# The loop over further token tiles of the experts moves from behind the first gather to behind the last expert

## The chip, the core and the metric

The kernel runs on one core of one Trainium2 chip. The metric is the device time of one execution in microseconds, of which the median over several runs is compared. The engines are TensorE (PE; its weight loads are PEld), VectorE (DVE), ScalarE (ACT), GpSimd (POOL) and SyncE (SP). [...]

## What is computed

Two blocks in a row, on 512 tokens of 1024 features. The first block has two layers: attention (a sliding window in layer 0, latent attention in layer 1), LayerNorm, a mixture of 32 experts, LayerNorm. The second block is a latent stream with a context stream beside it. The mixture is what matters here:

```python
def hier_moe(x, w_group, w_expert, w_gate, w_up, w_down):
    ...
    expert = (g_idx * M_PER_GROUP + e_idx).reshape(-1)      # two experts for each token
    order = jnp.argsort(expert)
    sizes = jnp.bincount(expert, length=M_EXPERTS)
    xs = xt[tok_sorted]
    hid = jax.nn.silu(lax.ragged_dot(xs, w_gate, sizes)) * lax.ragged_dot(xs, w_up, sizes)
    ys = lax.ragged_dot(hid, w_down, sizes) * weight
    return jax.ops.segment_sum(ys, tok_sorted, num_segments=n_tok)
```

512 tokens times 2 experts make 32 tokens for an expert on average.

## The kernel before

`moe(i, ...)` runs one mixture, for layer i = 0 and 1, and `_moe` is its body. The router's results on VectorE give, for each expert, the ranks of its tokens (`rkm`) and their number (`n_e`). Each expert has one tile of 64 token slots; two experts make a pair, and a loop over p = 0 to 15 works off the pairs. `ahead(p)` finds the token of each slot: one-hot matrices `oh` (L699, VectorE), small matmuls (L702), a sum and an addition (L706, L710) into `slots`, and a gather of the rows from DRAM (`xd`) into `x` on POOL (L756). `turn` transposes the rows (L767) and copies them to `xg` (L768). `gate_up` (L806), `turn_hidden` (L815) and `down` (L825) compute the experts, and `add_rows` (L742, POOL) adds their rows to `acc` in DRAM. The weights of a pair are twelve loads on SP (L863) into wide buffers `wx`, early ones `we`, spare ones `ws`, or granules `w`, a ring of three buffers of 512 KB that the other stages use too.

An expert with more than 64 tokens needs further tiles. Their number over all experts is `nov` (L783). Each engine reads it into a register (L892) and runs a loop that often (L893); its body finds the tile, gathers its rows and the expert's weights with indirect loads, and computes it. The loop closes a basic block on all five engines: what was traced ahead of it stands ahead of it in each queue, and what was traced behind it stands behind. Within a block a scheduler orders the instructions of each engine by a timeline of its own.

`meanwhile()` is the context stream, whose steps `fill` puts between the experts, on the right side of the memory, with its loads on POOL (L187). When the pairs are done, `acc` is read back as four row tiles (L979), and `combine` adds LayerNorm (L997, L305 to L309) and hands each tile on: in layer 0 to `mla_down`, which transposes it (L253) and multiplies with `b_w_down` (loaded at L189, split into two parts on ScalarE, L235, and VectorE, L236); in layer 1 to the second block, which transposes it at L1124 and multiplies with `w_in`.

```python
        ixs = []
        rows = [ahead(0)]                       # the first gather
        ...
        loaded = weights_of(0)
        ...
        with self.after("Pool")():
            n_over = nc.values_load(nov[0:1, 0:1], min_val=0, max_val=15)
        with tc.For_i(0, n_over, 1):
            ...
        rows += [ahead(p) for p in range(1, 3)]
```

Of the kernel before, what the change touches and what calls it, by code (L numbers as in the profile page):

```python
# [104 lines left out]
def bcast_rows(ap, n, parts=128):  # L105

    return bass.AP(tensor=ap.tensor, offset=ap.offset, ap=[[0, parts], [1, n]])


def finished(steps):  # L110

    while True:
        try:
            next(steps)
        except StopIteration as end:
            return end.value
# [13 lines left out]
class Net:  # L130
# [498 lines left out]
    def _moe(self, i, lg, meanwhile):  # L629
        nc, ins, tc = self.nc, self.ins, self.tc  # L630
# [109 lines left out]
        def add_rows(ix, y):  # L740

            nc.gpsimd.indirect_dma_start(out=acc, out_offset=bass.IndirectOffsetOnAxis(ap=ix, axis=0), in_=y, in_offset=None,  # L742
                                         bounds_check=1023, oob_is_err=False, compute_op=ALU.add)

        def targets_of(a, b):
            ix, w = targets([rkm[:, :, e] for e in range(a, b)], put[:, :, a:b], gone[:, a:b])
            return {e: (ix[:, e - a:e - a + 1], w[:, e - a:e - a + 1]) for e in range(a, b)}
# [3 lines left out]
        def rows_of(ix, n, rows=None):  # L751

            if rows is None:
                rows = ring.pop(0)
                ring.append(rows)
            nc.gpsimd.indirect_dma_start(out=rows[:n], out_offset=None, in_=self.xd,  # L756
                                         in_offset=bass.IndirectOffsetOnAxis(ap=ix[:n], axis=0), bounds_check=511,
                                         oob_is_err=False)
            return rows

        def turn(rows, n):

            xg = self.lp.tile([128, 8, 128], F32, name="xg")
            for g in range(2):
                ps = self.bank("tp", [128, 4, 128])
                for k in range(4):
                    nc.tensor.transpose(ps[:, k, :n], rows[:n, 4 * g + k::8], self.ident[:n, :n])  # L767
                (V.tensor_copy if g else nc.scalar.copy)(xg[:, 4 * g:4 * g + 4, :n], ps[:, :, :n])  # L768
            return xg

        def ahead(p):
            a = 1 if 0 < p < 4 else p // 4 * 4
            if a == p:
                b = 1 if p == 0 else p // 4 * 4 + 4
                ixs.append(slots([rkm[:, :, 2 * q:2 * q + 2] for q in range(a, b)], 2, past[:, a:b]))
            return rows_of(ixs[-1][:, p - a:p - a + 1], 128)


        more, ov, nof, nov = sm([128, 7, 32], "more"), sm([128, 32], "ov"), sm([128, 1], "nof"), sm([128, 1], "nov", I32)
# [18 lines left out]
        rows = [ahead(0)]  # L798

        def gate_up(hid, j, xg, wg, wu):  # L800

            ps = self.bank("sc")
            own, other = (slice(64 * a, 64 * a + 64) for a in (j, 1 - j))
            for k, ws in enumerate(zip(wg, wu)):
                for r, w in zip((other, own), ws):
                    nc.tensor.matmul(ps[r], xg[:, k], w, start=k == 0, stop=k == 7)  # L806
            nc.scalar.activation(hid[own], ps[other], AF.Silu)  # L807
            V.tensor_tensor(hid[own], hid[own], ps[own], op=ALU.mult)  # L808

        def turn_hidden(hid, rows=slice(0, 128)):  # L810

            n = rows.stop - rows.start
            tp = self.bank("tp", [128, 4, 128])
            for k in range(4):
                nc.tensor.transpose(tp[:, k, :n], hid[rows, k::4], self.ident[rows, rows])  # L815
            hT = self.lp.tile([128, 4, 128], F32, name="hT")
            V.tensor_copy(hT[:, :, :n], tp[:, :, :n])  # L817
            return hT

        def down(hT, wd, weight):  # L820

            py = self.bank("mm")
            for k, w in enumerate(wd):
                for h in range(2):
                    nc.tensor.matmul(py[64 * h:64 * h + 64], hT[:, k], w[:, 512 * h:512 * h + 512], start=k == 0, stop=k == 3)  # L825
            y = self.lp.tile([128, 512], F32, name="y")
            nc.scalar.activation(y, py, AF.Copy, scale=weight)  # L827
            return y

        def hidden():  # L830
            return self.lp.tile([128, 512], F32, name="hid")

        es = ExitStack()
# [18 lines left out]
        def weights_of(p):  # L852

            both = [([], [], []) for _ in range(2)]
            for j, n, h in [(j, n, h) for j in range(2) for h in range(2) for n in (0, 1)] + [(j, 2, h) for j in range(2) for h in range(2)]:
                e, ws = 2 * p + j, both[j]
                src, kk = ((w_g, 8), (w_u, 8), (w_d, 4))[n]
                parts, when = stream([128, kk // 2, 4096 // kk])
                k = h * kk // 2
                for w in parts:  # L860
                    m = w.shape[1]
                    with when():
                        nc.sync.dma_start(w, src[e].rearrange("(p k) f -> p k f", k=kk)[:, k:k + m])  # L863
                    k += m
                    ws[n].extend(w[:, a] for a in range(m))
            return both
# [2 lines left out]
        self.nstream = -1  # L869
        base, first, gen = (4, 99, 17) if i else (0, 6, 11)  # L870
        loaded = weights_of(0)

        tau = sm([128, 1], "tau")
        V.memset(tau, -1.0)
        oe, ob = sm([128, 32], "oe"), sm([128, 32], "ob")
# [12 lines left out]
        in_parts(put, we, tmp)  # L888
        past_half(gone, n_e)

        with self.after("Pool")():
            n_over = nc.values_load(nov[0:1, 0:1], min_val=0, max_val=15)  # L892
        with tc.For_i(0, n_over, 1):  # L893
            V.tensor_scalar(tau, tau, 1.0, None, op0=ALU.add)
            tiles_up_to(oe, ob)
# [19 lines left out]
            xg = turn(rows_of(slots([rko], 1)[:, 0:1], 64, self.granule([128, 1024])), 64)  # L915
# [15 lines left out]
            to, weight = targets([rko[:, :, 0]], one, go)  # L931
            hid = hidden()
            gate_up(hid, 1, xg[:, :, :64], picked("moe_w_gate", 8), picked("moe_w_up", 8))
            add_rows(to, down(turn_hidden(hid, slice(64, 128))[:, :, :64], picked("moe_w_down", 4), weight))
        rows += [ahead(p) for p in range(1, 3)]
        beside = meanwhile()
        instructions = nc.cur_bb.bb.instructions

        def fill(n):

            k = len(instructions)
            while n > 0:
                if next(beside, self) is self:
                    break
                n -= sum(a.engine == mybir.EngineType.PE for a in instructions[k:])
                k = len(instructions)

        for p in range(16):
            if p < 13:
                rows.append(ahead(p + 3))  # L950
            xg = turn(rows[p], 128)
            ws = weights_of(p) if p else loaded
            if p == 0:
                to = targets_of(0, 2)
            hid = hidden()
            for j in range(2):
                gate_up(hid, j, xg[:, :, 64 * j:64 * j + 64], *ws[j][:2])
            hT = turn_hidden(hid)
            for j in range(2):
                at, weight = to[2 * p + j]  # L960
                add_rows(at, down(hT[:, :, 64 * j:64 * j + 64], ws[j][2], weight))
                if p > 1:
                    fill(70 if i == 0 else 72)
            if p == 1 or (p == 0 and i == 0):
                es.close()
            if p == 0:
                to |= targets_of(2, 8)
            elif p % 4 == 3 and p < 15:
                to = targets_of(2 * p + 2, 2 * p + 10)
        loaded, added = self.after("SP"), self.after("Pool")  # L970
        finished(beside)
        xs, lnp = self.new_x(), self.wide([128, 2, 1024])
        with loaded():
            lnp = [lnp[:, a] for a in range(2)]
            for w, nm in zip(lnp, ("ln_g", "ln_b")):
                nc.sync.dma_start(w, bcast_rows(ins[nm][i, 1], 1024))
        for t, x in enumerate(xs):
            with added():
                nc.gpsimd.dma_start(x, self.acc[i][128 * t:128 * t + 128])  # L979
            added = self.after("Pool")  # L980
        return xs, lnp

    def wide(self, shape):
# [941 lines left out]
```

## Time and profile before

| what | value |
|---|---|
| three runs | 3419.17, 3430.11 and 3430.08 us; median 3430.08 |
| the profiled execution: its time | 3424.68 us |
| the profiled execution: its span | 3422.9 us |
| TensorE busy | 3139.3 us, 92% of the span |
| VectorE, ScalarE, POOL busy | 48%, 34%, 12% of the span |
| mean granted clock of TensorE | 0.959 of full speed |
| experts of layer 0, with their entry and exit | about 282 to 939 us |
| experts of layer 1, with their entry and exit | about 1210 to 1994 us |

All times of the trace count from the span's start. A row of the timeline has its start, its length, the engine (SPq is SP's queue), the line, the operation, what it writes and reads, and in brackets how long the engine had been idle and what ended that.

### The profile page before, as it was taken

Reading aid. Unit: us, or ns where it says so; the run is one execution under the profiler, and the core shown is the slowest. Engines: PE = TensorE matmul, PEld = TensorE weight load, DVE = VectorE, ACT = ScalarE, POOL = GpSimd, SP = SyncE. Lnnn points to the kernel's source line nnn. Section 1 sums busy time; section 2 is a strip of 40 time slices with the busy share of each in tenths; the row PEclk is TensorE's granted clock in tenths of the full one; section 3 lists DMA queues with packets and bytes.
Section 4 is the critical chain, followed back from the end, with each engine's and each line's share of the span. In section 5 each row is a group of like instructions: output and inputs, shape, how many; then the busy total and the mean of one; then the engine's idle time right before and its main releaser. Section 6 shows DMA issues by size and latency. Waiting matters only on the chain. (4 is left out here: it accounts for less than half of the span.)

```text
span 3422.9 us, 46600 instructions
## 1 busy us (share of the span) xinstructions
PE 3139.3 (92%) x17508; PEld 2123.4 (62%) x17508; DVE 1655.5 (48%) x4015; ACT 1172.2 (34%) x2322; POOL 406.2 (12%) x538
## 2 busy tenths in 40 slices
PE   8997999999699969999889759999999999999998
PEld 5454445544286636666445257767888777678887
DVE  3454242223266645555423056565555556755555
ACT  3331222222255324333122044344342442543332
POOL 0000221212100013232121100130000000400000
PEclk9998999999899979999999979999999999999999
DMA  8779989999931469888898932223233232333331
GB/s 287 264 272 351 352 327 338 364 355 388 329 121 43 165 225 379 317 321 314 302 359 322 387 99 80 76 74 111 87 99 98 81 92 67 81 100 93 97 94 56
DMA packets 282686, 716.01 MB, mean 209 GB/s; under 512 B 34936, under 2 KB 164008, under 8 KB 234584
## 3 DMA queue, kind: packets, MB, share of 16 engines
q1 hardware_dynamic: 250008, 634.80, 51.4%
q0 software_dynamic: 32448, 78.18, 7.4%
q8 instruction: 140, 2.29, 0.3%
q14 instruction: 90, 0.74, 0.1%
HBM read 691.76 MB, written 37.87 MB: 213 GB/s over the span
## 5 line engine op out<-in xcount | busy, mean ns | idle before, releaser
L236 DVE TENSOR_TENSOR wl<-w,wh 128x1024 fp32r<-128x1024 f32 (+4 forms) x467 | 437.1, 950 | 276.9 <-ACT wh L235 271.9
L235 ACT CAST wh<-w 128x1024 fp32r<-128x1024 f32 (+4 forms) x467 | 377.5, 827 | 512.5 <-PE po L242 116.2
L806 PE MATMUL sc<-wx,xg 128*64 128x512 f32 x1416 | 473.0, 613 | 23.1 <-DMA wx<-in_moe_w_up 16.9
L240 PE MATMUL mm<-xTh,wh 128*128 128x512 f32 (+1 forms) x672 | 263.3, 392 | 11.6 <-ACT xTh L235 6.1
L806 PEld LDWEIGHTS sc<-wx,xg 128*64 128x64 f32 x1416 | 133.0, 139 | 222.4 <-issue 176.9
L242 PE MATMUL mm<-xTh,wl 128*128 128x512 f32 (+1 forms) x672 | 262.2, 390 | 0.9 <-DVE wl L236 0.9
L241 PE MATMUL mm<-xTl,wh 128*128 128x512 f32 (+1 forms) x672 | 260.0, 387 | 0.0
L808 DVE TENSOR_TENSOR hid<-hid,sc 64x512 f32<-64x512 f32 x64 | 43.8, 685 | 304.7 <-ACT hid L807 304.4
L825 PE MATMUL mm<-wx,hT 128*64 128x512 f32 x704 | 173.7, 625 | 10.5 <-DVE hT L817 5.5
L807 ACT ACTIVATE hid<-sc 64x512 f32<-64x512 f32 x64 | 37.8, 591 | 382.5 <-PE sc L806 382.3
L806 PE MATMUL sc<-w,xg 128*64 128x512 f32 x352 | 168.0, 610 | 0.0
L742 POOL DMA_INDIRECT acc<-y,to x64 | 106.9, 1671 | 462.9 <-ACT y L827 262.1
L240 PEld LDWEIGHTS mm<-xTh,wh 128*128 128x128 f32 x672 | 127.9, 190 | 43.0 <-ACT xTh L235 6.6
L241 PE MATMUL sc<-xTl,wh 128*128 128x512 f32 (+1 forms) x384 | 146.0, 380 | 0.0
L242 PEld LDWEIGHTS mm<-xTh,wl 128*128 128x128 f32 x672 | 127.8, 190 | 28.8 <-DVE wl L236 1.3
L240 PE MATMUL sc<-xTh,wh 128*128 128x512 f32 (+1 forms) x384 | 145.6, 379 | 0.0
L242 PE MATMUL sc<-xTh,wl 128*128 128x512 f32 (+1 forms) x384 | 145.1, 378 | 0.0
L241 PEld LDWEIGHTS mm<-xTl,wh 128*128 128x128 f32 x672 | 127.7, 190 | 26.9 <-issue 0.7
L240 PE MATMUL a<-xTh,wh 128*128 128x256 f32 (+2 forms) x472 | 139.6, 296 | 4.7 <-ACT rs L1449 0.9
L240 PE MATMUL po<-wh,gTh 128*128 128x512 f32 x352 | 137.9, 392 | 3.8 <-DVE t2k L1771 2.8
L241 PE MATMUL po<-wl,gTh 128*128 128x512 f32 x352 | 137.1, 390 | 0.0
L242 PE MATMUL po<-wh,gTl 128*128 128x512 f32 x352 | 136.3, 390 | 0.0
(518 smaller groups left out, 6702.7 us busy)
## 6 DMA issues: line engine op xcount, KB each, us to landing
wx<-in_moe_w_up SPq DMA_DIRECT2D x89, 1024.0 KB
wx<-in_moe_w_down SPq DMA_DIRECT2D x88, 1024.0 KB
wx<-in_moe_w_gate SPq DMA_DIRECT2D x88, 1024.0 KB
g<-in_w_ada SPq DMA_DIRECT2D x48, 1024.0 KB
w<-in_ffn_w_up SPq DMA_DIRECT2D x176, 256.0 KB
w<-in_moe_w_gate SPq DMA_DIRECT2D x60, 512.0 KB
w<-in_ffn_w_up POOLq DMA_DIRECT2D x88, 256.0 KB
w<-in_ffn_w_down SPq DMA_DIRECT2D x44, 512.0 KB
```

Source lines behind the costliest of these rows:

```text
L235: self.nc.scalar.copy(hi, src)
L236: self.nc.vector.tensor_tensor(lo, src, hi.bitcast(F32), op=ALU.subtract)
L240: mm(ps, ah, bh, start=start, stop=False)
L241: mm(ps, ah, bl, start=False, stop=False)
L242: mm(ps, al, bh, start=False, stop=stop)
L742: nc.gpsimd.indirect_dma_start(out=acc, out_offset=bass.IndirectOffsetOnAxis(ap=ix, axis=0), in_=y, in_offset=None, bounds_check=1023, oob ...
L806: nc.tensor.matmul(ps[r], xg[:, k], w, start=k == 0, stop=k == 7)
L807: nc.scalar.activation(hid[own], ps[other], AF.Silu)
L808: V.tensor_tensor(hid[own], hid[own], ps[own], op=ALU.mult)
L825: nc.tensor.matmul(py[64 * h:64 * h + 64], hT[:, k], w[:, 512 * h:512 * h + 512], start=k == 0, stop=k == 3)
```

## The change

The loop, its reading of `nov` and the tensors of its body move as one block. They stood behind `past_half(gone, n_e)`, ahead of the second and third gather and of all experts; they now stand behind the last expert, behind the end of the context stream (`finished(beside)`) and the loads of the LayerNorm parameters, and ahead of the read-back of `acc`. The register load loses its place behind POOL's last instruction, and the four read-backs theirs (`added`). The body is the same word for word.

```diff
-        with self.after("Pool")():
-            n_over = nc.values_load(nov[0:1, 0:1], min_val=0, max_val=15)
-        with tc.For_i(0, n_over, 1):
-            V.tensor_scalar(tau, tau, 1.0, None, op0=ALU.add)
...
         rows += [ahead(p) for p in range(1, 3)]
         beside = meanwhile()
...
-        loaded, added = self.after("SP"), self.after("Pool")
+        loaded = self.after("SP")
         finished(beside)
         xs, lnp = self.new_x(), self.wide([128, 2, 1024])
         with loaded():
             lnp = [lnp[:, a] for a in range(2)]
             for w, nm in zip(lnp, ("ln_g", "ln_b")):
                 nc.sync.dma_start(w, bcast_rows(ins[nm][i, 1], 1024))
+
+        n_over = nc.values_load(nov[0:1, 0:1], min_val=0, max_val=15)
+        with tc.For_i(0, n_over, 1):
+            V.tensor_scalar(tau, tau, 1.0, None, op0=ALU.add)
...
         for t, x in enumerate(xs):
-            with added():
-                nc.gpsimd.dma_start(x, self.acc[i][128 * t:128 * t + 128])
-            added = self.after("Pool")
+            nc.gpsimd.dma_start(x, self.acc[i][128 * t:128 * t + 128])
         return xs, lnp
```

In the rows of the changed kernel the loop has the lines L933 and L934, the read-back L977, the store of a row tile L997.

VectorE at the entry of layer 0, before, from the one-hot of the first gather (`nov` is the number of further tiles, `slots` the gather's row numbers, `put` the routing weights for the adds):

```order
L699 TENSOR_TENSOR oh<-cst_2500,rkm 128x512
L783 CAST nov<-nof 128x1
L718 TENSOR_TENSOR tmp<-tmp,put 128x128
L706 TENSOR_REDUCE tk<-tp 128x1
L716 CAST put<-tmp 128x128
L710 TENSOR_TENSOR slots<-tk,past 128x1
L892 TENSOR_LOAD nov
L893 COMPARE_AND_BRANCH
```

The same place now:

```order
L699 TENSOR_TENSOR oh<-cst_2500,rkm 128x512 x2
L783 CAST nov<-nof 128x1
L718 TENSOR_TENSOR tmp<-tmp,put 128x128
L706 TENSOR_REDUCE tk<-tp 128x1
L699 TENSOR_TENSOR oh<-cst_2500,rkm 128x512
L710 TENSOR_TENSOR slots<-tk,past 128x1
L716 CAST put<-tmp 128x128
L699 TENSOR_TENSOR oh<-cst_2500,rkm 128x512
L726 TENSOR_TENSOR oh<-cst_2500,rkm 128x4x64
L706 TENSOR_REDUCE tk<-tp 128x3
```

The loop is gone from here, the one-hots of the second to fourth gather have come up, and two of them stand ahead of `slots`. Layer 1 has the same order at its entry.

SP at the exit of layer 0, before (`b_w_down` is what the next stage multiplies with):

```order
L863 DMA wx<-in_moe_w_down 128x2048
L189 DMA w<-in_b_w_down 128x2x384
L976 DMA wx<-in_ln_g 128x1024
L976 DMA wx<-in_ln_b 128x1024
L189 DMA w<-in_b_w_down 128x2x384 x3
L189 DMA w<-in_b_w_down 128x3x288 x2
L189 DMA w<-in_b_w_down 128x2x288
L1000 DMA xd<-x 128x1024 x4
```

The same place now:

```order
L863 DMA wx<-in_moe_w_down 128x2048
L931 DMA wx<-in_ln_g 128x1024
L931 DMA wx<-in_ln_b 128x1024
L934 COMPARE_AND_BRANCH
L934 UNCONDITIONAL_BRANCH x2
L1918 BRANCH_PREFETCH_HINT
L934 REGISTER_ALU
L934 COMPARE_AND_BRANCH
L934 UNCONDITIONAL_BRANCH
L189 DMA w<-in_b_w_down 128x2x384 x4
L189 DMA w<-in_b_w_down 128x3x288 x2
L997 DMA xd<-x 128x1024
```

All seven loads of `b_w_down` stand behind the loop. At the exit of layer 1 three loads of `w_in` (128x2x384 each) and two of constants (128x939 and 128x512) have moved behind it in the same way. At both entries, three granule loads `w` of expert weights that stood behind the loop on SP now stand ahead of its reading of `nov`, among the last stores of the stage before.

POOL at the exit of layer 0, before, with the entry of layer 1 behind it (L742 is the add into `acc`):

```order
L742 DMA acc_73<-y,to 1024x512
L187 DMA w<-in_w_out 128x2x256 x3
L742 DMA acc_73<-y,to 1024x512 x5
L979 DMA x<-acc_73 128x1024 x4
L756 DMA x<-xd,slots 128x1024
L892 TENSOR_LOAD nov
L893 COMPARE_AND_BRANCH
```

The same place now, from the end of the loop on:

```order
L742 DMA acc_73<-y,to 1024x512
L934 REGISTER_ALU
L934 COMPARE_AND_BRANCH
L934 UNCONDITIONAL_BRANCH
L977 DMA x<-acc_73 128x1024 x4
L756 DMA x<-xd,slots 128x1024 x4
L742 DMA acc_74<-y,to 1024x512 x2
```

The read-back stands behind the loop's last branch, the add above it is the one in the loop's body, and the four gathers of layer 1 follow each other.

## Rows read from the trace of the kernel before

**Rows 1.** The page's busy times: engine, busy us, share of the span, instructions.

```profile
PE 3139.3 (92%) x17508; PEld 2123.4 (62%) x17508; DVE 1655.5 (48%) x4015; ACT 1172.2 (34%) x2322; POOL 406.2 (12%) x538
```

**Rows 2.** Busy time of each engine by stretch, with granted clock and DMA share.

```profile
core 0: us, PE busy (x) PEld busy (x) DVE busy (x) ACT busy (x) POOL busy (x), PEclk, DMA share, GB/s
...
306.00:862.00 556.00, 523.92 (x3000) 260.40 (x2997) 167.66 (x388) 138.02 (x260) 111.65 (x119) 0.98 0.93 351
...
920.00:939.00 19.00, 0.34 (x2) 0.37 (x3) 7.17 (x16) 7.05 (x12) 3.76 (x5) 0.61 0.75 231
...
1237.00:1660.00 423.00, 415.16 (x2686) 267.52 (x2686) 214.38 (x458) 148.83 (x286) 132.79 (x158) 0.99 0.85 310
1660.00:1962.00 302.00, 263.16 (x1335) 119.84 (x1333) 75.36 (x185) 60.12 (x113) 46.84 (x46) 0.95 0.94 356
```

**Rows 3.** Timeline at the entry of layer 0.

```profile
291.71 0.69 DVE L699 TENSOR_TENSOR oh<-cst,rkm 128x512 bf16<-128x512 f32 x1
292.31 0.15 DVE L783 CAST nov<-nof 128x1 int32<-128x1 f32 x1
...
292.97 0.20 DVE L710 TENSOR_TENSOR slots<-tk,past 128x1 int32<-128x1 f32 x1
294.08 1.27 POOL L756 DMA_INDIRECT x<-xd,slots  x1 [293.65 <-DMA wx<-in_moe_w_up]
300.84 0.81 SPq L863 DMA_DIRECT2D w<-in_moe_w_gate  x2
301.27 1.90 DVE L699 TENSOR_TENSOR oh<-cst,rkm 128x512 bf16<-128x512 f32 x3 [8.10 <-issue]
...
303.35 1.95 PE L767 MATMUL tp<-cst,x 128*128 128x128 f32 x8
```

**Rows 4.** POOL's records of loop line L893: ns min/median/max, starts; both layers.

```profile
L893 POOLq INC_SWDGE_SEM  x1: 206/206/206, 299.8 to 299.8; - x1
...
L893 POOLq COMPARE_BRANCH  x1: 33/33/33, 301.6 to 301.6; - x1
...
L893 POOLq INC_SWDGE_SEM  x1: 967/967/967, 1229.4 to 1229.4; - x1
...
L893 POOLq COMPARE_BRANCH  x1: 33/33/33, 1231.6 to 1231.6; - x1
```

**Rows 5.** SP's waits at the entry of layer 0: us, times, longest.

```profile
SPq L893 <- remote: 6.4, 1, 6.4
```

**Rows 6.** Timeline at the entry of layer 1.

```profile
1224.04 1.07 POOL L756 DMA_INDIRECT x<-xd,slots  x1 [293.57 <-DVEq L893]
...
1234.18 1.12 PE L767 MATMUL tp<-cst,x 128*128 128x128 f32 x4 [0.26 <-DVE tk L706]
```

**Rows 7.** Timeline at the exit of layer 0.

```profile
915.82 10.84 SPq L189 DMA_DIRECT2D w<-in_b_w_down  x6
...
922.78 1.54 POOL L742 DMA_INDIRECT acc<-y,to  x1 [4.13 <-DMA acc<-y,to]
...
924.44 0.83 ACT L235 CAST wh<-w 128x768 fp32r<-128x768 f32 x1 [0.48 <-DMA w<-in_b_w_down]
...
928.25 2.22 POOL L979 DMA_DIRECT2D x<-acc  x4 [3.93 <-issue]
933.11 1.06 ACT L997 ACTIVATE wx<-x 128x1024 f32<-128x1024 f32 x1 [7.84 <-DMA x<-acc]
...
938.66 1.94 PE L253 MATMUL tp<-cst,x 128*128 128x128 f32 x8 [19.18 <-DVE ln_n L305]
```

**Rows 8.** Timeline at the exit of layer 1.

```profile
1968.84 0.59 POOL L979 DMA_DIRECT2D x<-acc  x1 [3.94 <-DMA acc<-y,to]
...
1972.66 1.06 ACT L997 ACTIVATE wx<-x 128x1024 f32<-128x1024 f32 x1 [9.59 <-DMA x<-acc]
```

**Rows 9.** Busy time by stretch, during the read-back of layer 0 alone.

```profile
930.50:935.00 4.50, 0.00 (x0) 0.00 (x0) 0.65 (x2) 1.67 (x3) 0.00 (x0) 0.50 1.01 401
```

**Rows 10.** The adds into `acc`, line L742, over the whole span.

```profile
L742 POOL DMA_INDIRECT acc<-y,to x64: 1542/1682/2057, 329.3 to 1963.3; - x64
```

More of the change, by code (lines that the diff above doesn't have):

```diff
@@ L889, in _moe, with fill @@
         past_half(gone, n_e)
-        with self.after("Pool")():
-            n_over = nc.values_load(nov[0:1, 0:1], min_val=0, max_val=15)
+        rows += [ahead(p) for p in range(1, 3)]
+        beside = meanwhile()
+        instructions = nc.cur_bb.bb.instructions
+        def fill(n):
+            k = len(instructions)
+            while n > 0:
+                if next(beside, self) is self:
+                    break
+                n -= sum(a.engine == mybir.EngineType.PE for a in instructions[k:])
+                k = len(instructions)
+        for p in range(16):
+            if p < 13:
+                rows.append(ahead(p + 3))
+            xg = turn(rows[p], 128)
+            ws = weights_of(p) if p else loaded
+            if p == 0:
+                to = targets_of(0, 2)
+            hid = hidden()
+            for j in range(2):
+                gate_up(hid, j, xg[:, :, 64 * j:64 * j + 64], *ws[j][:2])
+            hT = turn_hidden(hid)
+            for j in range(2):
+                at, weight = to[2 * p + j]
+                add_rows(at, down(hT[:, :, 64 * j:64 * j + 64], ws[j][2], weight))
+                if p > 1:
+                    fill(70 if i == 0 else 72)
+            if p == 1 or (p == 0 and i == 0):
+                es.close()
+            if p == 0:
+                to |= targets_of(2, 8)
+            elif p % 4 == 3 and p < 15:
+                to = targets_of(2 * p + 2, 2 * p + 10)
+        loaded = self.after("SP")
+        finished(beside)
+        xs, lnp = self.new_x(), self.wide([128, 2, 1024])
+        with loaded():
+            lnp = [lnp[:, a] for a in range(2)]
+            for w, nm in zip(lnp, ("ln_g", "ln_b")):
+                nc.sync.dma_start(w, bcast_rows(ins[nm][i, 1], 1024))
+        n_over = nc.values_load(nov[0:1, 0:1], min_val=0, max_val=15)
         with tc.For_i(0, n_over, 1):
@@ L934, in _moe @@
             add_rows(to, down(turn_hidden(hid, slice(64, 128))[:, :, :64], picked("moe_w_down", 4), weight))
[L935 to L969, printed above, removed]
-        loaded, added = self.after("SP"), self.after("Pool")
[L971 to L976, printed above, removed]
         for t, x in enumerate(xs):
-            with added():
-                nc.gpsimd.dma_start(x, self.acc[i][128 * t:128 * t + 128])
-            added = self.after("Pool")
+            nc.gpsimd.dma_start(x, self.acc[i][128 * t:128 * t + 128])
         return xs, lnp
```

## Prediction

> **What bounds the kernel now.** I read the page's busy shares first: TensorE is busy for 92% of the span [rows 1]. Such a mean hides its gaps, so the next view was busy time by stretch [rows 2]. Inside the two expert stages TensorE is nearly always at work: 523.92 of 556 us in layer 0, 415.16 of 423 us in the first part of layer 1, and 263.16 of 302 us in its last part, where the DMA share of 0.94 says that weights arrive about as fast as they are used. At each stage's two ends it stands almost still: from 920 to 939 us it works 0.34 of 19 us. The change touches these ends only, so the timelines there are the third view: the entry of layer 0 [rows 3], the loop's own branch records [rows 4], the entry of layer 1 [rows 6], and the two exits [rows 7, 8].
>
> At the entry TensorE waits for a chain: router on VectorE, slot numbers (`slots`), first gather on POOL, landing, transposes at L767. The loop of L893 stands in that chain. The reader is to see that no engine works between the slot numbers at 292.97 and 300.84, where SP issues again, and that VectorE's next step, one-hot number two, starts at 301.27 [rows 3]. The body never runs: the trace has 64 adds into `acc`, which is 2 layers x 32 experts and leaves none for the loop [rows 10]. So the price of the loop is its entry and exit alone, and the change moves that price from one place to another, twice.
>
> **What the loop costs where it stands.** POOL issues the gather at 294.08 and is through with it at 294.08 + 1.27 = 295.35. Its loop record of 299.8 is the first sign that the wait for the landing is over; its last branch is at 301.6, 1.8 us later. In layer 1 the same two records are at 1229.4 and 1231.6, 2.2 us apart [rows 4]. So passing the loop costs about 2.0 us after everything in flight has landed. The SP queue stood at the loop for 6.4 us [rows 5], and the three `w` loads behind it went out at 300.84. Behind the loop VectorE must still build the next one-hots, and TensorE's queue has their small matmuls ahead of L767; so the transposes start at 303.35, though the rows had landed by 299.8. In layer 1 they start at 1234.18 with the rows there by 1229.4 [rows 4, 6].
>
> **The change part by part: the two entries.** Without the loop here the one-hots and their matmuls run while the gather is under way, and L767 follows the landing at once. That would save 303.35 - 299.8 = 3.55 us and 1234.18 - 1229.4 = 4.78 us. The order of VectorE takes something back: two further one-hots now stand ahead of `slots`, the first before `nov`, the second behind `tk`. One lasts 0.69 us, and the next instruction starts about 0.6 us after it (291.71 to 292.31 for `nov` behind the first one); one of the two also covers time in which VectorE would have waited for TensorE's answer. I take 1.1 us for both. The gather then lands 1.1 us later. Layer 0 keeps 3.55 - 1.1 = 2.45 us, layer 1 keeps 4.78 - 1.1 = 3.68 us: **6.1 us saved**. Bounds: 8.3 us if the one-hots cost nothing, and 2.2 us if the gather lands a further 2 us later in each layer. The reason for that end: the three `w` loads (3 x 512 KB) now go out ahead of the gather, 1.6 MB, which at the 401 GB/s of [rows 9] are 3.9 us of the DMA engines' time, and the gather may have to wait for half of that.
>
> All else that moves at the entry costs nothing. Gathers two to four now issue one behind the other on POOL, which has no other work there. The register load of `nov` stays in SP's queue near its old place, so SP still waits for the router, but no longer for the gather. TensorE does the same steps in the same order. The gain passes through the stage, as the stage is bound by TensorE: the same matmuls start earlier, and buffers come free earlier by the same amount.
>
> **The interior.** In layer 0 the context stream falls a little behind the experts in TensorE's order and catches up before the end; in layer 1 only the last part is rearranged. TensorE's work is the same and its idle time in the layer 0 stretch is 556 - 523.92 = 32 us over sixteen pairs of experts [rows 2]. I take 0, with 3 us either way, a tenth of that idle time.
>
> **The two exits.** Before, the last add of layer 0 issues at 922.78 and lasts 1.54 us; POOL reads `acc` back at 928.25, 3.93 us after that, a wait for the add's landing that is needed in both kernels. The first row tile reaches ScalarE at 933.11 and TensorE starts at 938.66 [rows 7]. Now the loop stands between the landing and the read-back. POOL has to pass it after the landing, as it did at the entry: 2.0 us on the path, in each layer. Nothing hides it, for the whole chip waits for the read-back.
>
> The loop also holds back what overlapped this gap. In layer 0 six loads of `b_w_down` ran on SP from 915.82 for 10.84 us, during the last expert and the landing, with their casts (0.83 us) [rows 7]. All of `b_w_down` now stands behind the loop, and the first three loads of 384 KB, as many as the ring has buffers, fall beside the read-back of 4 x 512 KB. In layer 1 three loads of `w_in` and two of constants do the same (3 x 0.39 + 0.48 + 0.26 MB). What that adds lies between nothing, if the read-back is served as before, and the whole time of these loads at 401 GB/s [rows 9]: 1.2 MB are 3.0 us, 1.9 MB are 4.8 us. Only the first row tile is on the path, since the following ones are wanted some 4 us apart, a LayerNorm's length; so I stay in the lower half and take 1.3 us, once more the time of the first tile's own 0.52 MB. That makes 2.0 + 1.3 = 3.3 us for each exit, **6.6 us lost**. The casts I put at nothing in the middle value: the weights are issued before the read-back and ScalarE has idled there (7.84 us ahead of 933.11, [rows 7]); without that cover two casts ahead of the first LayerNorm step cost 1.7 us. Bounds: 4.0 us for both (the loop alone, 1.8 + 2.2), and 13.7 us: 2.0 + 3.0 + 1.7 in layer 0 and 2.2 + 4.8 in layer 1, if the read-back gets nothing until those loads are through.
>
> [...] No row of before shows these loads and the read-back at one time. [...]
>
> **Sum.** -6.1 + 6.6 = +0.5 us. The profiled execution has a span of 3422.9 us and a time of 3424.68, so 3425.2 for a like one of the changed kernel. The median of the three runs is 3430.08, 5.4 us above the profiled one, and they lie between 3419.17 and 3430.11; on the median's footing the sum is **3430.6 us**.
>
> **Rivals.** *Faster: both entry gaps go and the exit is hidden.* If the loop passes at the exit while the add is landing, the exit costs nothing and the sum is -6.1, or -8.3 at its bound: 3422 to 3424 us. For it: the engines other than POOL arrive early. Against it: at the entry the loop's last steps came after the landing in both layers [rows 4]. For over 0.5% (17 us) the whole stand from slots to transposes, less what the router still needs, would have to vanish in both layers, and the landing alone takes 4.4 us of it.
>
> *Slower: the held-back weights become the path.* Place: the exits. The six `b_w_down` loads took 10.84 us on SP, since a ring of three buffers admits the next load when a cast and a split are done. If TensorE's first projection waits for the fourth of them, then up to those 10.84 us stand behind the loop in series: 2.0 + 10.84 = 12.8 in layer 0, 2.2 + 4.8 = 7.0 in layer 1, less the 6.1 of the entries, +13.7 us: 3443.8 us. It decides when those weights are split later than the first row tile is transposed: 938.66 plus about 3 in the old time. For it: a cast of 0.83 us and a split have to run before the ring gives a buffer back, on the two engines that LayerNorm uses. Against: a tile needs 938.66 - 928.25 = 10.4 us from the read-back's issue to TensorE [rows 7], and four loads of 0.39 MB are 3.9 us of transfer.
>
> *The change moves the loop but not the wait.* If SP's register load, or the gather itself, still sets the first transposes, the entries give nothing: 3430.1 + 6.6 = 3436.7 us. Against it stands that the rows lay ready 3.55 and 4.78 us before the transposes, and that the order has nothing of the loop left between them.
>
> **How the numbers follow.** About 0.5% is what a measurement of this kernel can tell from no change. The forecast (between -3 and +7 us) gets 0.62, the faster rival 0.14, the slower one 0.14, the unmoved wait 0.10. All of these prices lie within 17 us of 3430; half of each of the first two rivals' chance I keep for a like effect that is larger than priced. So faster by more than 0.5% gets 0.07, slower by more 0.08 (the slower rival's end lies nearest to the line), and within 0.85. The range: the best sum is -8.3 + 4.0 - 3 = -7.3, the worst -2.2 + 13.7 + 3 = +14.5; runs lie up to 11 us below their median and nearly none above, and half of that is added below: **3417 to 3444 us**.
>
> **What would show it.** Right: in the changed trace TensorE starts L767 about 301 and 1230.5 us; POOL's read-back comes some 6 us after the last add's descriptors instead of 3.9; TensorE's gap at the exit of layer 0, 19 us before, grows to some 22; the stage lengths between are within 3 us of before. Wrong: `b_w_down` named as the releaser of the first projection, a new wait at the first expert's weights, or interior stretches that differ by more than the ends do.

## The result: 12 us slower, and half of it where no step was priced

| | before | after |
|---|---|---|
| median of 7 runs each | 3428.07 us | 3440.39 us |
| lowest and highest | 3419.17 and 3430.11 us | 3437.2 and 3448.01 us |
| the profiled execution: time, span | 3424.68, 3422.9 us | 3440.16, 3438.4 us |

The ratio is 1.0053, with a 95% interval of 1.004 to 1.0065. The prediction had put 0.85 on "within 0.5%" at 3430.6 us; the median lies 9.8 us above that, inside the range of 3417 to 3444 us. That the range holds it is in part luck: two errors at the entries cancel, and 8.6 us come from a part that was priced at nothing. The kernel is slower, by about the amount that can just be told.

The two traces, cut at the same instructions, show where. "Low" is the part of a stretch in which the trace has TensorE at the lower granted clock (0.50; the only other level in both traces is 1.00). Length less half of it is an estimate of what the stretch would take at the upper level, for work that TensorE bounds: for the second block it gives 1389.6, 1389.2 and 1390.5 us in three executions with 74 to 100 us low.

| stretch | before | after | difference | low, before and after |
|---|---|---|---|---|
| start to the router's first step (L651) | 283.1 | 284.3 | +1.2 | |
| entry of layer 0, from there to the first expert matmul | 22.6 | 22.3 | -0.3 | |
| experts of layer 0, first L806 to last L825 | 613.2 | 614.2 | +1.0 | 28.1 and 12.9 |
| exit of layer 0, from there to L253 | 19.8 | 25.0 | +5.2 | |
| latent attention | 274.5 | 274.2 | -0.3 | 21.9 and 21.6 |
| entry of layer 1 | 23.9 | 18.1 | -5.8 | |
| experts of layer 1 | 724.7 | 726.1 | +1.4 | 42.2 and 44.0 |
| exit of layer 1 | 25.0 | 31.2 | +6.2 | |
| second block | 1426.7 | 1433.6 | +6.9 | 74.2 and 88.8 |

At the upper clock the experts of layer 0 took 599.2 us before and 607.8 after, **8.6 us more**, which the clock hides in this pair of executions; and the second block took 1389.6 and 1389.2, so that its 6.9 us are clock alone. Entries, exits and layer 0 are the change: -0.3 - 5.8 + 5.2 + 6.2 + 8.6 = +13.9 us, against 12.3 us between the medians and 15.5 us between the two profiled spans.

The page of the changed kernel, first its busy times (as [rows 1]), then busy time by stretch (as [rows 2]):

```profile
PE 3148.5 (92%) x17508; PEld 2125.9 (62%) x17508; DVE 1655.5 (48%) x4015; ACT 1170.1 (34%) x2320; POOL 406.9 (12%) x538
```

```profile
306.00:862.00 556.00, 523.95 (x3014) 261.76 (x3015) 169.01 (x389) 139.37 (x261) 110.60 (x117) 0.99 0.93 349
920.00:939.00 19.00, 1.32 (x7) 0.18 (x3) 1.92 (x2) 2.37 (x4) 4.28 (x6) 0.60 0.51 134
1237.00:1660.00 423.00, 415.17 (x2688) 267.95 (x2688) 213.58 (x456) 149.98 (x286) 131.94 (x156) 0.99 0.86 308
1660.00:1962.00 302.00, 263.83 (x1328) 118.85 (x1328) 76.15 (x186) 60.01 (x113) 46.50 (x46) 0.94 0.94 353
```

TensorE's share is unchanged and nothing here looks wrong: these stretches are cut by time, and the losses lie in what is done in them. The timelines of the two entries, layer 0 first (as [rows 3] and [rows 6]):

```profile
296.04 1.36 POOL L756 DMA_INDIRECT x<-xd,slots  x1 [295.60 <-DVE oh L699]
...
304.18 1.94 PE L767 MATMUL tp<-cst,x 128*128 128x128 f32 x8 [7.93 <-DMA x<-xd,slots]
```

```profile
1231.64 1.15 POOL L756 DMA_INDIRECT x<-xd,slots  x1 [296.96 <-DVE oh L699]
...
1235.24 1.09 PE L767 MATMUL tp<-cst,x 128*128 128x128 f32 x4 [3.40 <-DMA x<-xd,slots]
```

L767 now waits for the gather and nothing else. In layer 1 it starts 1235.24 - 1232.79 = 2.45 us after POOL is through with the gather, in layer 0 304.18 - 297.40 = 6.78 us after. The traces' landing times tell why: in all four entries the gather lands shortly behind the last weights that SP had issued ahead of it. Before, these landed at 299.44 and 1227.46 and the gather at 299.75 and 1229.15; now they land at 303.87 and 1234.16 and the gather at 304.04 and 1235.11. Next the exits (as [rows 7] and [rows 8]); in layer 1 only the read-back and the first LayerNorm step:

```profile
924.50 1.54 POOL L742 DMA_INDIRECT acc<-y,to  x1 [4.00 <-DMA acc<-y,to]
931.48 11.68 SPq L189 DMA_DIRECT2D w<-in_b_w_down  x6
932.44 2.24 POOL L977 DMA_DIRECT2D x<-acc  x4 [6.40 <-issue]
...
938.98 1.06 ACT L994 ACTIVATE wx<-x 128x1024 f32<-128x1024 f32 x1 [2.06 <-DMA x<-acc]
...
940.95 0.83 ACT L235 CAST wh<-w 128x768 fp32r<-128x768 f32 x1 [0.82 <-DMA w<-in_b_w_down]
...
941.68 1.14 ACT L306 ACTIVATE wx<-x,ln_n 128x1024 f32<-128x1024 f32 x1
```

```profile
1974.02 2.22 POOL L977 DMA_DIRECT2D x<-acc  x4 [6.20 <-issue]
...
1981.56 1.06 ACT L994 ACTIVATE wx<-x 128x1024 f32<-128x1024 f32 x1 [16.06 <-DMA w<-in_w_in]
```

The read-back is issued 6.40 and 6.20 us after the end of POOL's record of the last add, which the prediction calls the add's descriptors (3.93 and 3.94 before), its first tile reaches ScalarE 6.54 and 7.54 us later (4.86 and 3.82 before). In both layers that is the landing of this tile, 938.95 and 1981.54, though the second row names a load of `w_in`. In layer 0 a cast of `b_w_down` now stands ahead of the second LayerNorm step.

### The profile page after: what moved, and what is told of

Read it like the earlier page. It is cut to its first block, busy times and chain, and to the rows that moved or that the text cites. A ratio compares the mean times of both kernels' runs of the same rounds, so it can differ in the third digit from the quotient of the medians.

```text
span 3438.4 us, 46545 instructions
## 1 busy us (share of the span) xinstructions
PE 3148.5 (92%) x17508; PEld 2125.9 (62%) x17508; DVE 1655.5 (48%) x4015; ACT 1170.1 (34%) x2320; POOL 406.9 (12%) x538
## 5 line engine op out<-in xcount | busy, mean ns | idle before, releaser
L236 DVE TENSOR_TENSOR wl<-w,wh 128x1024 fp32r<-128x1024 f32 (+4 forms) x467 | 436.0, 948 | 283.1 <-ACT wh L235 275.6
L806 PE MATMUL sc<-wx,xg 128*64 128x512 f32 x1416 | 475.9, 607 | 20.0 <-DMA wx<-in_moe_w_up 12.0
L240 PE MATMUL mm<-xTh,wh 128*128 128x512 f32 (+1 forms) x672 | 263.4, 392 | 11.6 <-ACT xTh L235 6.1
L806 PEld LDWEIGHTS sc<-wx,xg 128*64 128x64 f32 x1416 | 134.7, 138 | 217.5 <-issue 175.4
L825 PE MATMUL mm<-wx,hT 128*64 128x512 f32 x704 | 175.2, 627 | 10.1 <-DVE hT L817 4.7
L806 PE MATMUL sc<-w,xg 128*64 128x512 f32 x352 | 168.1, 610 | 0.0
L742 POOL DMA_INDIRECT acc<-y,to x64 | 107.2, 1674 | 472.3 <-ACT y L827 316.5
```

The lines of the kernel that those rows point to most:

```text
L236: self.nc.vector.tensor_tensor(lo, src, hi.bitcast(F32), op=ALU.subtract)
L240: mm(ps, ah, bh, start=start, stop=False)
```

## The experiments

The times beside each experiment are medians; the kernel before had 3425.7 to 3427.0 us in the runs beside them.

**No loop at all.** Edit: the loop and its register load are gone.

```diff
-        with self.after("Pool")():
-            n_over = nc.values_load(nov[0:1, 0:1], min_val=0, max_val=15)
-        with tc.For_i(0, n_over, 1):
...
```

> The kernel before without the loop and without the load of its count: further tiles of an expert with more than 64 tokens are left out (none occurs in these inputs). It measures the whole price of the loop. Theory from the two traces: at the entry of layer 1 the loop costs 6.1 us (1234.18 - 1222.97 from slots to transposes, 11.2 us, against 4.6 in the changed kernel, less 0.5 for the further one-hots), at the entry of layer 0 nothing that lasts, since that stage is fed by its weights and the first gather lands later there: 3428 - 6 = 3422 us, with transposes of layer 1 about 5 to 6 us after slots and POOL's read-back 4 us after the last add as before. The prediction's own steps: 2.45 + 3.68 = 6.1 us too, but with 2.5 of it in layer 0. Rival, the loop's entry is hidden by something else that comes late: 3428 us and unchanged rows.

Measured: 3432.14 us over 12 runs, ratio 1.0016 (1.0 to 1.0031), so not faster, and 10 us over the expectation. The entry of layer 1 is 18.2 us long, 5.7 less than before, as expected, and the exits are 19.8 and 26.1. But layer 0's experts took 625.6 us with 41.6 of them low: 604.8 at the upper clock, 5.6 more than before. This kernel has no loop that could cost anything there. So the loss inside layer 0 comes from taking the loop away from its old place, and not from putting it behind the last expert.

**One layer at a time.** Edit: the loop as a function, called at the front in one layer and behind the last expert in the other.

```diff
+        if i == 0:        # only_l1; in only_l0: i == 1
+            further()
...
+        if i != 0:
+            further()
```

> The loop stands behind the last expert in layer 1 alone; layer 0 has it behind the first gather as before. Theory from the two traces: entry of layer 1 -6.1 us, exit of layer 1 +5.7 us (2.3 for passing the loop, 3.4 for the read-back beside constants and w_in), so -0.4: 3426 to 3430 us. Rival, the late rows of the changed trace that lie outside the four places (last expert of layer 1 2.4 us later, second block 6.5 us longer) follow from the move in layer 1: -0.4 + 8.9 = 3436 to 3437 us. The prediction's steps: -3.7 + 3.3 = 3427.7.

> The loop stands behind the last expert in layer 0 alone; layer 1 as before. Theory from the two traces: the entry of layer 0 gains nothing that lasts, the exit costs 5.4 us (2.5 for the loop, 1.7 for the read-back beside b_w_down, 1.2 for a cast ahead of the first LayerNorm step), perhaps 1 us more while TensorE's granted clock is low behind the gap: 3433 to 3435 us. The prediction's steps: -2.45 + 3.3 = 3429. Rival, the gain of layer 1's entry seen in the changed trace was only the catching up of layer 0's loss: then most of the loss vanishes at layer 1's entry, 3428 to 3429.

Measured: only layer 1 moved, 3429.6 us (ratio 1.0011, 0.9997 to 1.0026), entry 18.1, exit 30.9, layer 0 596.7 at the upper clock: the first theory. Only layer 0 moved, 3445.7 us (1.0066, 1.0046 to 1.0087), 11 us over its highest expectation: the exit cost 25.8 - 19.8 = 6.0, and layer 0's experts, which I had still put at nothing, 606.3 at the upper clock, +7.1. The change in layer 1 is about a draw; the change in layer 0 makes the whole loss.

**The loop ahead of the first gather.** Edit: in both layers the loop stands ahead of `rows = [ahead(p) ...]`, all three gathers behind it.

```diff
-        ixs = []
-        rows = [ahead(0)]
...
+        ixs, rows = [], []
+        rows += [ahead(p) for p in range(3)]
```

> The loop stands ahead of the first gather in both layers, where POOL's software queue is empty, and the read-back is as before. Theory: passing a loop costs about 2 us behind the emptied software queue, and the rest of its price is the wait for the landing and the steps held back behind it; ahead of the gather only the 2 us stay, and the gather, the next one-hots and the transposes follow without it. Entry of layer 1: 6.1 - 2.2 = about 4 us earlier than before, layer 0 nothing that lasts: 3423 to 3425 us. Rival, the loop waits for all loads in flight, SP's weights among them: the gather goes later by several us in layer 0, where the DMA share is 0.92, and the kernel is not faster: 3428 to 3434.

Measured: 3441.43 us (1.0044, 1.0027 to 1.0061), 7 us over the rival's range. Its mechanism held: the entries take 28.2 and 26.0 us, 5.6 and 2.1 more than before. Layer 0's experts take 604.2 us at the upper clock, which the rival had not counted. The view is the DMA engines' traffic in forty slices from 1215 to 1235 us (busy tenths, GB/s), of the kernel before, of the changed one and of this one, and then SP's wait at the loop:

```profile
DMA  9999999999999999999999864200000000767999
...
DMA  9999999510986799999999999989999999994853
...
DMA  0096979999999999999999999999500000009789
```

```profile
SPq L888 <- DMA we<-in_moe_w_gate: 3.5, 1, 3.5
```

With the loop, in either place, the DMA engines run empty for some 4 us at the end of this stretch; without it they are full there. In this kernel no gather is in flight, and all engines stand at the loop from 1224.7 (`nov`) to 1232.05: 6.6 us until the last **weight** has landed (1231.24), and 0.8 us more. So the loop waited for every load in flight, SP's weights among them. In the kernel before, the gather was the last of these loads in both layers; POOL's wait at the loop in layer 1 ended at 1229.18, just behind the landing at 1229.15, so [rows 4] were read rightly.

**The loss inside layer 0.** Windows over pairs 3 to 9, from the first L806 of pair 3 to that of pair 10, of before, after, no loop and only layer 1 (us, TensorE's busy time and matmuls, ..., granted clock, DMA share):

```profile
393.93:696.49 302.56, 286.73 (x1769) 156.97 (x1768) 97.40 (x210) 73.39 (x136) 65.45 (x73) 0.98 0.93 353
...
391.59:699.10 307.51, 293.40 (x1770) 158.04 (x1769) 96.17 (x208) 71.70 (x134) 66.04 (x73) 0.99 0.94 349
...
390.36:700.64 310.28, 296.36 (x1770) 159.34 (x1769) 96.13 (x208) 71.83 (x134) 65.48 (x73) 0.98 0.93 347
...
392.76:696.53 303.77, 288.83 (x1770) 158.56 (x1769) 97.29 (x210) 73.43 (x136) 65.61 (x73) 0.97 0.93 352
```

The same matmuls, the same DMA share, and TensorE is *busy* 6.7 us longer at a higher clock; no idle row shows it. The gate and up matmuls of an expert tell why. Their busy time alone in these windows (TensorE, then its weight loads), before and after:

```profile
393.93:696.49 302.56, 115.87 (x448) 33.36 (x448) 0.98 0.93 353
...
391.59:699.10 307.51, 124.23 (x449) 37.00 (x449) 0.99 0.94 349
```

That is 8.4 us more for the same matmuls. First expert of pair 7 on TensorE, before, then after:

```profile
573.41 3.65 PE L806 MATMUL sc<-wx,xg 128*64 128x512 f32 x16
577.00 0.44 PE L1411 MATMUL a<-cst,t2k 128*128 128x128 f32 x2
577.37 3.65 PE L806 MATMUL sc<-wx,xg 128*64 128x512 f32 x16
```

```profile
562.49 1.07 PE L806 MATMUL sc<-wx,xg 128*64 128x512 f32 x2
563.49 0.39 PE L240 MATMUL a<-xTh,wh 128*128 128x256 f32 x1
...
566.56 3.65 PE L806 MATMUL sc<-wx,xg 128*64 128x512 f32 x14
570.14 0.44 PE L1408 MATMUL a<-cst,t2k 128*128 128x128 f32 x2
570.51 1.07 PE L806 MATMUL sc<-wx,xg 128*64 128x512 f32 x2
571.51 0.39 PE L240 MATMUL a<-xTh,wh 128*128 128x256 f32 x1
```

A matmul leaves two records: the 14 experts of pairs 3 to 9 have 14 x 16 gate and up matmuls and 448 records. Gate writes one half of the PSUM rows and up the other, and neighbours of the two kinds run side by side, their records starting 0.01 us apart (788.25 and 788.26 us before): 16 records, eight matmuls, take 3.65 us. A matmul that stands alone between context matmuls takes 1.07 us for its two. Where the context stream cuts a run after an odd number, two matmuls are left alone: 2 and 14 records take 1.07 + 3.65 us where 16 took 3.65, so 1.1 us more. Pairs 3 to 9 have some 13 such lone couples before and 20 after (counted by the starts of their records); 7 x 1.1 = 7.7 us. At the upper clock these pairs took 302.8 to 304.1 us in the six kernels that have the new order, and 295.1 to 295.7 in four executions with the old one: the kernel before twice, the loop moved in layer 1 alone, and a kernel below. The experts ahead of pair 3 and behind pair 9 took the same in both groups, within the spread of each (83.7 to 84.4 and 216.6 to 219.9 us). So the whole loss of layer 0 lies where the lone couples were added.

**Gate and up exchanged.** Cuts fall after an odd number because up's weights are loaded behind gate's. Edit, on the kernel before and on the changed one:

```diff
-                for r, w in zip((other, own), ws):
+                for r, w in list(zip((other, own), ws))[::1 if i == 0 and j and k < 4 else -1]:
```

> The kernel before with the order of the gate and up matmuls of one step exchanged, but for the first half of the second expert of a pair in layer 0. By the order of the instructions the context stream then cuts 6 steps of layer 0 and 1 of layer 1 between gate and up, where the kernel before has 27 and 30. Theory from the traces: uncut, the two matmuls of a step start 0.01 us apart and the step takes 0.43 us, cut they run one after the other and the step takes about 1.0 us more; so up to 21 us are saved in layer 0, where loads may take some of it back, and up to 29 us in layer 1: 3380 to 3405 us. Rival, the stages are bound by their weights or the matmuls' pairing costs nothing: 3425 to 3430 us.

> The changed kernel with the same exchange of gate and up; 7 cuts in layer 0 and 1 in layer 1, where the changed kernel has 31 and 32. Theory: the cuts were what the changed kernel lost inside layer 0 (7 us at full clock), so against p_before_pairs only entries and exits are left: +0.8 - 5.8 + 5.2 + 6.2 = +6.4 us, half of the 12.3 us seen, and both are 25 us or more below their originals. Rival, the loss inside layer 0 has another cause (weights that come later behind the entry): then the difference stays at 12 us or more.

(These texts count the cuts between gate and up, 27 and 30 before; lone couples, of which the exchange leaves some 7 in layer 0 and 1 in layer 1 of either kernel, are the better count. And an uncut step takes 0.86 us, not 0.43.) Measured: 3400.31 us (0.9923, 0.9893 to 0.9953) and 3401.22 us (0.9926, 0.9901 to 0.9952). Both beat both originals by 24 us or more, and **the difference between the two places of the loop can no longer be seen**. With some 10 us of interval the medians can't tell 0.9 us from the 6.4 us that the expectation left for entries and exits; but the rows show that the loss inside layer 0 is gone: its experts take 596.6 and 593.4 us at the upper clock, the entries 23.8 and 18.3 in layer 1, the exits 20.6, 25.9 and 25.3, 30.3. The windows over the experts of layer 0 and of layer 1, first of the kernel before, then exchanged, and last gate and up alone in layer 1, before and exchanged:

```profile
305.68:918.88 613.20, 571.54 (x3223) 280.56 (x3222) 177.25 (x403) 145.73 (x272) 116.65 (x122) 0.98 0.93 353
1237.02:1961.69 724.67, 677.99 (x4018) 387.36 (x4019) 289.74 (x641) 208.93 (x399) 179.60 (x204) 0.97 0.89 329
```

```profile
304.50:919.42 614.92, 557.50 (x3224) 277.38 (x3220) 177.63 (x403) 148.36 (x274) 118.38 (x122) 0.97 0.92 351
1238.11:1927.33 689.22, 645.55 (x4020) 378.81 (x4019) 289.75 (x641) 209.50 (x399) 178.84 (x204) 0.97 0.93 346
```

```profile
1237.02:1961.69 724.67, 272.76 (x1024) 79.99 (x1024) 0.97 0.89 329
...
1238.11:1927.33 689.22, 241.54 (x1024) 72.38 (x1024) 0.97 0.93 346
```

Layer 1 gets 35 us shorter, and gate and up are busy 31 us less in it. In layer 0 TensorE is busy 14 us less and the stage no shorter: idle time takes it back. TensorE's waits for weights grow from 6.7 to 11.6 us; its other waits were not taken apart. Two more kernels, the exchange in layer 1 alone (`[::-1 if i else 1]`) and the exchange in both layers without the loop:

> The kernel before with gate and up exchanged in layer 1 alone: 27 cut steps in layer 0 as before, none in layer 1 (30 before). Theory: a cut step costs 1.0 us where TensorE sets the pace, so layer 1 gets 29 to 36 us shorter, and layer 0, where the exchange in both layers brought nothing because loads took it back, keeps its length: 3392 to 3402 us, as fast as with the exchange in both layers. Rival, the gain of the exchange came from other things that moved with it: over 3410 us.

> The kernel before without the loop (further tiles are left out; none occurs in these inputs) and with gate and up exchanged in both layers; 7 and 1 cut steps, as in the changed kernel with the exchange. Theory: without the loss by cuts what the loop costs shows as it is, 5 to 6 us in the entry of layer 1 and little in layer 0: 3392 to 3396 us against 3400 with the loop in either place. Rival, the loop costs nothing wherever it stands: 3400 us.

Measured: 3394.55 us (0.9886, 0.9862 to 0.9909), layer 1 692.4 us: as far as the interval tells, the exchange in layer 1 is all that counts, and this is the lowest median of a complete kernel here. Without the loop 3389.8 us (0.9893, 0.9869 to 0.9917); it can't be told from 3394.55, so neither its theory nor its rival is shown.

**A second loop.** Edit, on the changed kernel, right behind the loop:

```diff
+        with tc.For_i(0, n_over, 1):
+            V.memset(tau, -1.0)
```

> The changed kernel with a second, nearly empty loop right behind the first, at the exit of each layer; it never runs either. Theory: passing a loop costs 2.3 us of instructions on all engines behind an emptied software queue, so POOL's read-back comes 8.7 us after the last add's descriptors (6.4 in the changed kernel, 3.9 before), in each layer: +4.6 us, 3445 us. Rival, the loop's price is the wait for the landing alone, which the read-back needs anyway: the second one costs under 0.5 us, 3440 us, and the read-back stays at 6.4.

```profile
933.83 2.23 POOL L979 DMA_DIRECT2D x<-acc  x4 [7.83 <-issue]
1971.62 2.21 POOL L979 DMA_DIRECT2D x<-acc  x4 [7.04 <-issue]
```

Measured: 3440.08 us over 10 runs. The read-back comes 1.43 and 0.84 us later than with one loop. Neither theory holds: a bare pass costs about 1.1 us, and the other half of the 2.3 to 2.5 us comes with the first loop only. POOL's records of the first loop have an `INC_SWDGE_SEM` (as in [rows 4]) of 0.89 and 0.52 us that the second lacks; the rest of that half is not taken apart.

**The weights behind the read-back.** Edit, on the changed kernel: `b_w_down` is loaded on POOL's queue behind the read-back.

```diff
+        if self.behind:
+            with self.behind():
+                self.nc.gpsimd.dma_start(out, src)
```

> The changed kernel with the loads of b_w_down in POOL's queue behind the read-back of layer 0, not in SP's beside it. Theory: the read-back's first tile, which reached ScalarE 6.5 us after its issue in the changed kernel (6.1 to 7.7 us in the four kernels with a loop in this place, 4.2 to 6.2 us in the six without), is slowed by these loads; behind it they leave it 4.2 to 5.2 us, and the cast no longer stands ahead of the first LayerNorm step. Layer 1's exit, unchanged, stays at 6.5 to 7.5 us. The time as a whole may be lost again, since the weights then come later: 3435 to 3445 us. Rival, the read-back is slow because it is issued right behind the loop or beside the adds' traffic: 6 us or more in layer 0 as well.

```profile
936.72 2.24 POOL L984 DMA_DIRECT2D x<-acc  x4 [6.28 <-issue]
...
940.33 1.06 ACT L1001 ACTIVATE wx<-x 128x1024 f32<-128x1024 f32 x1 [13.73 <-DMA x<-acc]
```

Measured: 3444.94 us. The first tile takes 3.6 us instead of 6.5 and no cast stands in its way; layer 0's exit shrinks from 25.0 to 20.6 us, layer 1's stays at 30.0. So the held-back loads slowed the read-back in layer 0; for layer 1 this was not tried. The latent attention behind it takes 278.1 us instead of 274.2, of which 2 us are low clock (25.6 and 21.6 us low); the other 2 may be its weights, which come later.

**The kernel before once more.**

> The kernel before, profiled once more. The second block, from the first transposes behind layer 1 to the last matmul, took 1426.7 us before and 1433.6 us in the changed kernel, with 74.2 and 88.8 us of it at half the granted clock; the four other kernels had 77.5 to 107.9 us and lengths that fit 1389 us plus half of the time at half clock. Theory: that time belongs to the execution, not to the change; so the same kernel gives another value here, by 5 us or more, and length minus half of it is 1388 to 1391 again. Rival: it belongs to the kernel, then it is 74 us again, within 2 us.

```profile
1986.67:3413.39 1426.72, 1368.22 (x7164) 1093.82 (x7164) 825.66 (x1643) 563.54 (x981) 96.94 (x194) 0.97 0.30 86
...
1973.24:3413.51 1440.27, 1379.71 (x7163) 1100.45 (x7164) 825.95 (x1643) 563.67 (x981) 96.52 (x194) 0.97 0.29 85
```

The second block of one kernel: 1426.7 us with 74.2 low, and now 1440.3 with 99.6 low; 1390.5 at the upper clock. Everything ahead of it was 13.4 us earlier this time, and the spans are the same by chance. The low time belongs to the execution, and stretches of two traces have to be compared with it taken out.

## Why the prediction was wrong, point by point

- **The body never runs; the loop alone is moved.** Right: 64 adds in the changed trace as in [rows 10].
- **Passing the loop costs 2.0 us.** Right in size at the exits, +2.47 and +2.26; "some 6 us instead of 3.9" is what the rows show. Of it about 1.1 us is the bare pass.
- **Entry of layer 0, 2.45 us saved.** Wrong: 0.3. L767 came at 304.18 and not about 301. The gather takes 8.0 us from issue to landing where it took 5.7: the weights ahead of it land later, and the DMA engines are busy for 0.98 of that time, 0.80 before. The prediction named this effect and kept it for its bound, 2 us (with it, its lower bound for both entries is 2.1 us and not 2.2).
- **Entry of layer 1, 3.68 us saved.** Mis-sized: 5.8. The wait behind the landing went as predicted (5.0 us before, 0.1 now), and the one-hots cost 0.9 us; but the gather also takes 3.5 us from issue to landing where it took 5.1. It is luck that the errors of the two entries cancel: 6.1 us saved together, as predicted.
- **The exits, 3.3 us each.** Right in kind, the term of the held-back loads too small: 5.2 and 6.2 us, inside the bounds of 4.0 and 13.7 for both. The first tile was 1.7 and 3.7 us later where I took 1.3, and the cast that I put at nothing cost layer 0 1.3 us (938.98 to 941.68, against 933.11 to 934.48). The 1.3 us, and that these loads slow the read-back at all, were my estimate, as no row of before shows the two at one time; in layer 0 the first tile took 3.6 us without the loads of `b_w_down` and 6.5 us beside them.
- **The interior, 0 with 3 us either way.** This is the step that failed. I saw that the context stream stood elsewhere in TensorE's order, counted the same matmuls and the same idle time, and priced the new order at nothing. But what a gate or up matmul cost hung on its neighbours, eight side by side taking 3.65 us and one alone 1.07: 7 more lone couples, 7.7 us, and layer 0 took 8.6 us more. It is the sign of being wrong that the prediction had named, an interior that differs by more than the ends do (8.6 against 5.3 us).
- **The sum.** By these rows -6.1 + 11.4 + 8.6 = +13.9 us instead of +0.5; the medians lie 12.3 us apart. Of the rivals, the slower one named the exits, which made 11.4 of it; but `b_w_down` did not become the releaser of the first projection, which waited 0.88 us for its own cast of the row tile.

Open stay two things. Why the scheduler, with the block no longer closed behind the first gather, sets the context stream at other places was not tried. And part of the difference is clock whose cause is not shown. With the levels 1.00 and 0.50, the span of an execution times its mean granted clock is its length less half its low time, and the record has both for every execution: on average 3292.5 us in 7 executions of the changed kernel and 3284.8 in 24 of the kernel before, with 296 and 280 us of low time (283 and 289 in 17 and 13 others of the kernel before). So 7.7 of the 15.6 us between these mean spans is work and waiting at the upper clock, and 8 us comes with 16 us more of low time. In the two profiled executions the entries and exits have 7.4 us more of it; the rest may be the spread between executions.

## What to carry to other kernels

Moving a barrier moves more than its wait: it changes what a scheduler may interleave, so compare the order inside the stages, neighbour by neighbour, where matmuls run in couples as gate and up do here (eight in 3.65 us, one alone in 1.07). The loop here never ran and still waited for the loads in flight, 6.6 us of them ahead of the first gather of layer 1, so for a place ask first what is being loaded there. Before two traces are compared by stretch, take out the time at the lower granted clock (74.2 and 99.6 us in the second block of one kernel); and look for a loss also in busy time: the same gate and up matmuls of seven pairs were busy 115.9 and 124.2 us here.

## What the runs showed of the hardware

- Gate and up matmuls, which write two halves of the PSUM rows, start 0.01 us apart, and eight of them in couples take 3.65 us; one alone between other matmuls takes 1.07 us. The loss shows as busy time: 115.9 and 124.2 us for the same matmuls of seven pairs. Taking most cuts out of layer 1 gave 35 us of 725.
- Ahead of the first gather of layer 1 the loop stood 6.6 us for weights in flight, with no gather issued, and 0.8 us more to pass; at the exits, behind a loop, a second one cost 1.43 and 0.84 us.
- A gather of 0.5 MB landed 3.5 to 8.0 us after its issue, and in all four entries 0.2 to 1.7 us behind the last weights issued ahead of it; a first row tile took 3.6 us without and 6.5 us beside 1.2 MB of loads.
- The same 7164 matmuls of the second block ran 74.2 to 107.9 us at the lower granted clock in different executions, which by half of the difference is an estimated 17 us of time.
